# An encoder layer's MLP up stage: products issued as two row tiles of 64 contraction rows

## The chip, the core and the metric

The kernel runs on one core of a Trainium2 chip. The metric is the device time of one execution in microseconds; the profile is one further execution, recorded by the hardware profiler. TensorE (PE in the profile, its weight loads PEld) multiplies into PSUM, a memory of eight banks of 512 fp32 columns on 128 partitions. ScalarE (ACT) and VectorE (DVE) read those banks; GpSimd (POOL) works between buffers of the on-chip memory; SyncE (SP) issues most transfers. Each engine takes its instructions in order.

## What is computed

A layer with two attention branches, followed by a squared-ReLU MLP, for 256 prompt rows and 1024 sample rows of width 1024:

```python
def _layer(x, rel_bias, g_mix, w_in, b_gate, w_branch_a, w_branch_b, w_out, sink, g_mlp, w_up, w_down):
    ...
    x = x + merged @ w_out
    h = _rmsnorm(x, g_mlp)
    return x + jnp.square(jax.nn.relu(h @ w_up)) @ w_down
```

The change is in `h @ w_up`: 1280 rows, 1024 deep, 4096 columns wide.

## The kernel before

Every product is made from operands that are split in a high and a low part of the type fp32r: `hi` is a copy rounded to fp32r (ACT), `lo` is the rest (DVE), and three products, hi by lo, lo by hi and hi by hi, are added up in one PSUM bank. `split_steps` makes such a pair, `six` issues the three products of each piece of 128 contraction rows. Each product loads 128 x 128 weights and passes 512 columns, or 256 for the prompt.

The sample rows go through seven block products in place of eight, each of half depth and half width (the names A11, A12, S1 to S4 and A22 are its combined operands); the prompt's 256 rows are multiplied in the plain way.

The up stage is 16 calls of `up`, called units 0 to 15 here, each for 256 columns of `w_up`. A unit holds seven **runs** of twelve products of 512 columns, made by `seven`, and two prompt sums of 24 products of 256 columns, made by `prompt`. In an ordinary unit PE's order is: A11 into bank x; A12 into y; the prompt's first sum; S2 into x, on top of what is there; S3 into z; S1 into x; A22 into z; S4 into x; the prompt's second sum. Between two runs into the same bank, the sum so far is read out:

- c1: after A11, ACT copies x; `relu2_sum` adds c1 to y on DVE and squares its positive part: the quarter u11.
- c2: after S2, ACT copies x. c7: after S3, ACT copies z.
- u22 is x after S1 plus c7; u21 is z after A22 plus c2 (both on DVE); u12 is x after S4 alone (`relu2`, two ACT instructions).
- the prompt's sums go through `relu2` in halves of 128 columns.

POOL then forms four sums of the quarters, S1 to S4 (L1986 to L1989), and SP stores seven buffers u, which are there once each: the next unit's u11 waits until POOL's third sum has read the old one. Meanwhile the weights of the next unit are prepared by `right_pair`: POOL subtracts to ta and tb (DVE does it for unit 1), ACT makes whi and DVE wlo of four weight tiles per unit, of 128 x 1024 elements. These steps stand between the runs, where `steps_of` takes them from a generator; within one engine the order is that of the program. Unit 0 does more: its hooks (`entering`) split the combined activations (chi on ACT, clo on DVE) and turn the last prompt tile, and it issues the first two runs of unit 1 ahead of its own S4. The last unit's hooks split the first operands of the down stage (dhi and dlo).

PSUM is one pool of eight banks under four tags: three mm, two sc, two pt, one pv. The sum x takes one of mm, y of pt, z of sc, the prompt pv and sc. The down stage, `down.go()`, sums into dn in all eight.

Of the kernel before, what the change touches and what calls it, by code (L numbers as in the profile page):

```python
# [10 lines left out]
F32 = mybir.dt.float32  # L11
F32R = mybir.dt.float32r
AF = mybir.ActivationFunctionType
ALU = mybir.AluOpType
# [83 lines left out]
def encoder_kernel(  # L98
# [25 lines left out]
    psum = ctx.enter_context(tc.tile_pool(name="psum", bufs=1, space=PSUM))  # L124
    narrow, narrows = ExitStack(), []

    def slot(name, shape=(P, D), dt=F32):
# [201 lines left out]
    def turned(t, tags=("pt", "pt")):  # L329

        banks = []
        for h in range(2):
            ps = bank(tags[h], "tr")
            for i in range(4):
                k = 4 * h + i
                nc.tensor.transpose(ps[:, P * i : P * (i + 1)], xn[t][:, P * k : P * (k + 1)], ident)  # L336
            banks.append(ps.rearrange("p (i q) -> p i q", i=4))
        del xn[t]
        return banks

    def six(ps, lefts, rights, first, last, mid=None):

        seq = [x for (lh, ll), (rh, rl) in zip(lefts, rights) for x in ((rl, lh), (rh, ll), (rh, lh))]
        for i, (a, b) in enumerate(seq):
            nc.tensor.matmul(ps, a, b, start=first and i == 0, stop=last and i == len(seq) - 1,  # L345
                             skip_group_check=True)
# [586 lines left out]
    if True:  # L933
# [16 lines left out]
        class Rows:  # L950
# [5 lines left out]
            def begin(self):  # L956
                self.z = stage("long", (P, T), n=4)
# [938 lines left out]
    with ExitStack() as pre:  # L1896
        late = pre.enter_context(tc.tile_pool(name="stage", bufs=1))

        def stage(name, n, bufs=1):
            return late.tile([P, n], F32, name=name, tag=name, bufs=bufs)  # L1900

        def relu2(out, ps):
            nc.scalar.activation(out, ps, AF.Relu)
            nc.scalar.activation(out, out, AF.Square)  # L1904

        def relu2_sum(out, ps, other):
            nc.vector.tensor_tensor(out, ps, other, op=ALU.add)
            nc.vector.scalar_tensor_tensor(out, out, 0.0, out, op0=ALU.max, op1=ALU.mult)

        def begin(parts):  # L1910

            x, y = bank("mm", "x"), bank("pt", "y")
            seven(x, A11, parts[0], 0, last=False)
            c1 = stage("c1", 512)
            nc.scalar.activation(c1, x, AF.Copy)
            yield
            seven(y, A12, parts[0], 1)
            yield x, y, c1

        begun = {}  # L1920
        stores_u = []

        def store_u():
            while stores_u:
                nc.sync.dma_start(*stores_u.pop(0))

        def up(j, b, parts, hooks):

            def prompt_out(ps, dst):
                for i, d in enumerate(dst):
                    relu2(d[:, 512:], ps[:, P * i : P * i + P])

            start = begin(parts)
            if j not in begun:
                next(start)
            z = bank("sc", "z")
            nb = np_ = None
            steps_of(b, 2)  # L1940
            next(hooks, None)
            store_u()
            u = [stage(f"u{i}", TH) for i in range(7)]
            u11, u12, u22, u21 = u[A11], u[A12], u[A22], u[S3]
            x, y, c1 = begun[j] if j in begun else next(start)
            relu2_sum(u11[:, :512], y, c1)
            steps_of(b, 2)
            if j:
                pa = prompt(parts[0])
# [7 lines left out]
            nc.scalar.activation(c2, x, AF.Copy)  # L1957
# [6 lines left out]
            nc.scalar.activation(c7, z, AF.Copy)  # L1964
            if not j:
                steps_of(nb, 2)
            next(hooks, None)
            seven(x, S1, parts[2], 0, False, False)
# [4 lines left out]
            seven(z, A22, parts[2], 1, False)  # L1973
            relu2_sum(u21[:, :512], z, c2)
            next(hooks, None)
            if not j:
                *_, begun[1] = begin(np_)
            seven(x, S4, parts[3], 1, False)
            relu2(u12[:, :512], x)
            next(hooks, None)  # L1980
            if not j:
                steps_of(nb, 4)
                prompt_out(prompt(parts[0]), (u11, u21))
                steps_of(nb, 2)
            prompt_out(prompt(parts[3], "sc"), (u12, u22))
            nc.gpsimd.tensor_tensor(u[S1], u21, u22, op=ALU.add)  # L1986
            nc.gpsimd.tensor_tensor(u[S2], u[S1], u11, op=ALU.subtract)
            nc.gpsimd.tensor_tensor(u[S3], u11, u21, op=ALU.subtract)
            nc.gpsimd.tensor_tensor(u[S4], u12, u[S2], op=ALU.subtract)  # L1989
            stores_u.extend((scr_u[j // 4][:, i, j % 4, :], u[i]) for i in (A11, S1, A22, S2, S3, A12, S4))  # L1990
            next(hooks, None)
            return nb, np_

        def entering():

            run(halves(S3, combined[S3]))
            yield
            run(turn_prompt(9, ("pt", "sc")))
# [8 lines left out]
            yield  # L2007

        b = b0, p0
# [6 lines left out]
        store_u()  # L2016

    down.go()


# [22 lines left out]
```

## Time and profile before

| | |
|---|---|
| median of 3 runs | 1674.7 us (1674.65 to 1675.09) |
| span of the profiled execution, first to last instruction | 1672.7 us |
| granted TensorE clock | 1.000 |
| products (PE), of them in the up stage | 9256, 2112 (84 + 48 in each of 16 units) |
| HBM read, written | 175.13 MB, 90.92 MB |
| waits of PE in the up stage longer than 0.1 us | one, 0.2 us, at its start |

The profile puts a product's record from its start to its modelled end, and products are pipelined: a record of 0.39 us stands every 0.23 us. So the pace is read from the starts. A row of the timeline is: start, length, engine, line, operation, output and inputs, shapes, number of merged instructions, and in brackets how long the engine stood idle before and on what it waited. ACT, DVE and POOL records are lengths that can be added up.

### The profile page before, as it was taken

How to read it: one execution, taken by the hardware profiler on the slowest of the kernel's cores; microseconds unless marked ns; L12 is line 12 of the kernel's file. 1: busy time of each engine (PE TensorE's matmuls, PEld its weight loads, DVE VectorE, ACT ScalarE, POOL GpSimd, SP SyncE). 2: the span in 40 equal slices, each digit the busy share in tenths (PEclk: the TensorE clock that was granted, in tenths of full speed). 3: DMA queues.
4: the chain of work that ended last, by engine and by line, in shares of the span. 5: the costliest groups of instructions: out<-in, count | busy, mean ns of one | idle time of the engine just before them, and what ended most of it. 6: DMA issues, size and time to landing. Idle time of an engine off the chain costs nothing.

```text
span 1672.7 us, 24767 instructions
## 1 busy us (share of the span) xinstructions
PE 1661.8 (99%) x9256; PEld 1413.9 (85%) x9256; DVE 951.1 (57%) x1534; ACT 714.3 (43%) x1473; POOL 494.3 (30%) x372
## 2 busy tenths in 40 slices
PE   9999999999999999999999999999999999999998
PEld 7898888888888888888888888888888888888886
DVE  6732233455654565667278545445456775867665
ACT  6232323345654655654176333333334333333435
POOL 1212222111112352100100656455554250514240
PEclk9999999999999999999999999999999999999999
DMA  7416552666667794845121443343356934733333
GB/s 256 150 54 126 134 132 75 165 196 189 198 184 228 192 236 134 284 135 193 38 89 59 161 160 120 121 161 125 116 191 230 362 113 137 253 104 107 120 120 126
DMA packets 224176, 262.45 MB, mean 157 GB/s; under 512 B 29486, under 2 KB 153694, under 8 KB 224056
## 3 DMA queue, kind: packets, MB, share of 16 engines
q1 hardware_dynamic: 217000, 242.69, 45.4%
q0 software_dynamic: 6720, 17.65, 5.1%
q8 instruction: 73, 1.20, 0.3%
q10 hardware_dynamic: 336, 0.53, 0.1%
q14 instruction: 47, 0.39, 0.1%
HBM read 175.13 MB, written 90.92 MB: 159 GB/s over the span
## 4 chain that ended last, share of the span: by engine, by line
PE 96%; ACT 2%; DVE 1%; DMA 1%; issue 0%; SPq 0%; DVEq 0%; ACTq 0%
PE dn L345 22%; PE x L345 19%; PE mm L192 14%; PE z L345 10%; PE v L819 6%; PE y L345 5%; PE mm L345 5%; PE pv L345 3%; PE sc L345 3%; PE pt L1193 2%; PE pv L1209 2%; PE sc L553 1%; PE pv L600 1%; PE pt L586 1%; PE tr L336 1%; PE sc L1167 1%
## 5 line engine op out<-in xcount | busy, mean ns | idle before, releaser
L345 PE MATMUL dn<-dhi,ulo 128*128 128x512 f32 x448 | 174.3, 389 | 0.0
L345 PE MATMUL dn<-dlo,uhi 128*128 128x512 f32 x448 | 174.3, 389 | 0.0
L345 PE MATMUL dn<-dhi,uhi 128*128 128x512 f32 x448 | 174.3, 389 | 0.0
L345 PE MATMUL x<-chi,wlo 128*128 128x512 f32 x424 | 166.5, 393 | 0.0
L345 PE MATMUL x<-clo,whi 128*128 128x512 f32 x424 | 165.6, 390 | 0.0
L345 PE MATMUL x<-chi,whi 128*128 128x512 f32 x424 | 165.0, 389 | 0.0
L312 DVE TENSOR_TENSOR wlo<-ta,whi 128x1024 fp32r<-128x1024 f32 x30 | 56.3, 1876 | 174.0 <-ACT whi L310 174.0
L312 DVE TENSOR_TENSOR wlo<-raw,whi 128x1024 fp32r<-128x1024 f32 x60 | 89.6, 1494 | 103.1 <-ACT whi L310 98.2
L391 POOL TENSOR_TENSOR tb<-raw 128x512 f32<-128x512 f32 x25 | 32.3, 1290 | 363.7 <-DMA raw<-in_w_in_dram 111.8
L345 PEld LDWEIGHTS dn<-dhi,ulo 128*128 128x128 f32 x448 | 84.1, 188 | 17.6
L345 PEld LDWEIGHTS dn<-dhi,uhi 128*128 128x128 f32 x448 | 84.1, 188 | 17.4
L345 PEld LDWEIGHTS dn<-dlo,uhi 128*128 128x128 f32 x448 | 84.1, 188 | 17.4
L345 PEld LDWEIGHTS x<-chi,whi 128*128 128x128 f32 x424 | 79.6, 188 | 17.1
L345 PEld LDWEIGHTS x<-chi,wlo 128*128 128x128 f32 x424 | 79.8, 188 | 15.1
L345 PEld LDWEIGHTS x<-clo,whi 128*128 128x128 f32 x424 | 79.8, 188 | 14.6
L1735 POOL TENSOR_TENSOR t<-raw,t 128x1024 f32<-128x1024 f32 x16 | 46.4, 2924 | 149.2 <-DMA raw<-in_w_down_dram 149.2
L186 DVE TENSOR_TENSOR ulo<-uraw,uhi 128x1024 fp32r<-128x1024 f32 x56 | 86.1, 1558 | 4.4 <-ACT uhi L185 4.4
L1886 DVE TENSOR_TENSOR v<-v,dn 128x512 f32<-128x512 f32 x90 | 59.7, 683 | 42.3 <-PE dn L345 42.3
L186 DVE TENSOR_TENSOR dlo<-raw,dhi 128x1024 fp32r<-128x1024 f32 x32 | 50.1, 1590 | 46.3 <-ACT dhi L185 45.3
L1986 POOL TENSOR_TENSOR u<-u,u 128x640 f32<-128x640 f32 x16 | 25.1, 1569 | 173.3 <-ACT u L1904 173.3
L345 PE MATMUL dn<-dhi,up 128*128 128x512 f32 x224 | 73.5, 389 | 0.0
L345 PE MATMUL z<-chi,wlo 128*128 128x512 f32 x184 | 71.6, 389 | 0.0
(319 smaller groups left out, 4619.2 us busy)
## 6 DMA issues: line engine op xcount, KB each, us to landing
scr_u<-u SPq DMA_DIRECT2D x112, 320.0 KB, 2.6
uraw<-scr_u SPq DMA_DIRECT2D x56, 512.0 KB, 3.9
raw<-in_w_down_dram SPq DMA_DIRECT2D x36, 512.0 KB, 6.7
raw<-in_w_up_dram SPq DMA_DIRECT2D x32, 512.0 KB, 5.2
raw<-in_w_in_dram SPq DMA_DIRECT2D x25, 512.0 KB, 5.2
sg<-scr_g SPq DMA_DIRECT2D x32, 256.0 KB, 6.2
uraw<-scr_u SPq DMA_DIRECT2D x28, 256.0 KB, 4.5
qk<-scr_kb SPq DMA_DIRECT2D x48, 128.0 KB, 2.6
```

The costliest lines, as they stand in the source:

```text
L186: nc.vector.tensor_tensor(lo, src, hi.bitcast(F32), op=ALU.subtract)
L192: nc.tensor.matmul(ps, a, b, start=i == 0, stop=i == len(seq) - 1)
L312: nc.vector.tensor_tensor(lo, src, hi.bitcast(F32), op=ALU.subtract)
L336: nc.tensor.transpose(ps[:, P * i : P * (i + 1)], xn[t][:, P * k : P * (k + 1)], ident)
L345: nc.tensor.matmul(ps, a, b, start=first and i == 0, stop=last and i == len(seq) - 1, skip_group_check=True)
L391: (nc.vector if vector else nc.gpsimd).tensor_tensor(o, x, y, op=ALU.subtract)
L819: nc.tensor.matmul(ps[:, :n], a, b, start=k == 0 and j == 0, stop=k == KC - 1 and j == 2)
L1193: nc.tensor.transpose(ps[:, P * k : P * k + P], s[:, h, P * b : P * b + P], ident)
L1209: nc.tensor.matmul(pv[HALVES[h], P * i : P * i + P], src, pt[:, at + 2 * b + h, :], start=b == 0, stop=b == W // P - 1, skip_group_check=True)
L1735: nc.gpsimd.tensor_tensor(o, a, b, op=ALU.subtract)
L1886: nc.vector.tensor_tensor(v, v, ps, op=ALU.add)
L1986: nc.gpsimd.tensor_tensor(u[S1], u21, u22, op=ALU.add)
```

## The change

Three things change. A product of 128 contraction rows becomes two products of 64 rows, one on the upper half of the array's rows and one on the lower, issued one after the other, each into a bank of its own (`tiled`). A sum therefore lies in two banks, and is joined where it is read: `closed` copies the first bank on ACT and adds the second on DVE; `relu2_sum` has a second add. And PSUM is held in three pools, one after the other: the old one up to the up stage, one of four double banks a to d in it, and the old layout again for the down stage; a table, HOMES, gives each sum its double bank by unit.

```diff
+    def both_banks(tag, name):
+        return psum.tile([P, 2, 512], F32, name=name, tag=tag, bufs=1)
...
+    def tiled(ps, lefts, rights, n, first, last):
+
+        seq = [x for (lh, ll), (rh, rl) in zip(lefts, rights) for x in ((rl, lh), (rh, ll), (rh, lh))]
+        for i, (a, b) in enumerate(seq):
+            for h, rows in enumerate(HALVES):
+                nc.tensor.matmul(ps[:, h, :n], a[rows, :], b[rows, :], start=first and i == 0,
+                                 stop=last and i == len(seq) - 1, skip_group_check=True)
...
+        def closed(out, ps, n=512):
+
+            nc.scalar.activation(out, ps[:, 0, :n], AF.Copy)
+            nc.vector.tensor_tensor(out, out, ps[:, 1, :n], op=ALU.add)
...
         def relu2_sum(out, ps, other):
-            nc.vector.tensor_tensor(out, ps, other, op=ALU.add)
+            nc.vector.tensor_tensor(out, ps[:, 0, :], other, op=ALU.add)
+            nc.vector.tensor_tensor(out, out, ps[:, 1, :], op=ALU.add)
             nc.vector.scalar_tensor_tensor(out, out, 0.0, out, op0=ALU.max, op1=ALU.mult)
...
+        HOMES = ({"x": "a", "y": "c", "z": "d", "p": "d", "q": "a"}, {"x": "b", "y": "c", "p": "d", "z": "a", "q": "c"},
+                 {"x": "d", "y": "a", "p": "b", "z": "c", "q": "a"})
...
             def prompt_out(ps, dst):
+                c = stage("cp", NP)
+                closed(c, ps, NP)
                 for i, d in enumerate(dst):
-                    relu2(d[:, 512:], ps[:, P * i : P * i + P])
+                    relu2(d[:, 512:], c[:, P * i : P * i + P])
...
-            seven(x, S2, parts[1], 0, False, False)
+            seven_tiled(x, S2, parts[1], 0, False, False)
             c2 = stage("c2", 512)
-            nc.scalar.activation(c2, x, AF.Copy)
+            closed(c2, x)
...
-            seven(z, S3, parts[1], 1, last=False)
+            z = home_of(j, "z")
+            seven_tiled(z, S3, parts[1], 1, last=False)
             c7 = stage("c7", 512)
-            nc.scalar.activation(c7, z, AF.Copy)
+            closed(c7, z)
...
-            seven(x, S4, parts[3], 1, False)
-            relu2(u12[:, :512], x)
+            seven_tiled(x, S4, parts[3], 1, False)
+            closed(u12[:, :512], x)
+            relu2(u12[:, :512], u12[:, :512])
```

How the instructions move is shown at three places. A name in brackets is what the row waits for.

PE, the beginning of z's second run (A22) in the last unit, with the end of x's run S1 ahead of it; x and z are the PSUM sums, chi and clo the split activations, whi and wlo the split weights. Before:

```order
L345 MATMUL x<-clo,whi 128x512
L345 MATMUL x<-chi,whi 128x512
L345 MATMUL z<-chi,wlo 128x512 [waits Activation_49]
L345 MATMUL z<-clo,whi 128x512
L345 MATMUL z<-chi,whi 128x512
```

With the change:

```order
L366 MATMUL x<-clo,whi 128x512 x2
L366 MATMUL x<-chi,whi 128x512 x2
L366 MATMUL z<-chi,wlo 128x512 [waits DVE_49]
L366 MATMUL z<-chi,wlo 128x512
L366 MATMUL z<-clo,whi 128x512 x2
L366 MATMUL z<-chi,whi 128x512 x2
```

Each product stands there twice, once per tile, and the run's first product, which writes z again, waits for DVE where it waited for ACT.

DVE, the middle of an ordinary unit, from u11 to the low parts of the next weights. Before:

```order
L1907 TENSOR_TENSOR u_10420<-y,c_10406 128x512 [waits DMAHW2_49,PE_49,Pool_49]
L1908 SCALAR_TENSOR_TENSOR u_10420<-u_10420 128x512 [waits DVE_49]
L312 TENSOR_TENSOR wlo<-tb,whi 128x1024 [waits Activation_49]
L312 TENSOR_TENSOR wlo<-raw,whi 128x1024 [waits DMAHW1_49,PE_49,Activation_49]
L1907 TENSOR_TENSOR u_10425<-x,c_10508 128x512 [waits DMAHW4_49,PE_49,Activation_49]
L1908 SCALAR_TENSOR_TENSOR u_10425<-u_10425 128x512 [waits DVE_49]
```

With the change:

```order
L1931 TENSOR_TENSOR u_12009<-y,c_11995 128x512 [waits DVE_49,DMAHW4_49,PE_49,Pool_49]
L1932 TENSOR_TENSOR u_12009<-u_12009,y 128x512 [waits DVE_49]
L1933 SCALAR_TENSOR_TENSOR u_12009<-u_12009 128x512 [waits DVE_49]
L322 TENSOR_TENSOR wlo<-tb,whi 128x1024 [waits Activation_49]
L1924 TENSOR_TENSOR c_12124<-c_12124,x 128x512 [waits Activation_49]
L1924 TENSOR_TENSOR cp<-cp,p 128x256 [waits Activation_49]
L322 TENSOR_TENSOR wlo<-raw,whi 128x1024 [waits DMAHW3_49,Activation_49]
L1924 TENSOR_TENSOR c_12163<-c_12163,z 128x512 [waits Activation_49]
L1931 TENSOR_TENSOR u_12014<-x,c_12163 128x512 [waits DMAHW6_49,DVE_49,PE_49]
```

Three closings are new there: c2 (from x), the prompt's (cp, from p) ahead of the low part of raw, and c7 (from z) behind it.

DVE, the beginning of unit 1, from the low part of ta to the low part of raw. Before:

```order
L312 TENSOR_TENSOR wlo<-ta,whi 128x1024 [waits DVE_49,Activation_49]
L312 TENSOR_TENSOR wlo<-tb,whi 128x1024 [waits PE_49,Activation_49]
L1907 TENSOR_TENSOR u_9421<-y,c_9309 128x512 [waits DMAHW5_49,Pool_49]
L1908 SCALAR_TENSOR_TENSOR u_9421<-u_9421 128x512 [waits DVE_49]
L312 TENSOR_TENSOR wlo<-raw,whi 128x1024 [waits Activation_49]
```

With the change:

```order
L1924 TENSOR_TENSOR cp<-cp,p 128x256 [waits Activation_49]
L322 TENSOR_TENSOR wlo<-ta,whi 128x1024 [waits Activation_49]
L1924 TENSOR_TENSOR cp<-cp,q 128x256 [waits DVE_49,Activation_49]
L322 TENSOR_TENSOR wlo<-tb,whi 128x1024 [waits DVE_49,Activation_49]
L1931 TENSOR_TENSOR u_9594<-y,c_9402 128x512 [waits DMAHW5_49,Pool_49]
L1932 TENSOR_TENSOR u_9594<-u_9594,y 128x512 [waits DVE_49]
L1933 SCALAR_TENSOR_TENSOR u_9594<-u_9594 128x512 [waits DVE_49]
L322 TENSOR_TENSOR wlo<-raw,whi 128x1024 [waits Activation_49]
L1924 TENSOR_TENSOR c_9685<-c_9685,x 128x512 [waits Activation_49]
```

Unit 0's two prompt closings (cp from p and from q) now stand around the low part of ta, and unit 1's closing of x (c from x) stands behind u11's three operations, the first of which waits for POOL.

More of the change, by code (lines that the diff above doesn't have):

```diff
@@ L123, in encoder_kernel, with open_banks @@
     slots = ctx.enter_context(tc.tile_pool(name="slots", bufs=N_M))
-    psum = ctx.enter_context(tc.tile_pool(name="psum", bufs=1, space=PSUM))
+    psums = [ctx.enter_context(ExitStack()) for _ in range(3)]
+    def open_banks(i):
+        if i:
+            psums[i - 1].close()
+        return psums[i].enter_context(tc.tile_pool(name=f"psum{i}", bufs=1, space=PSUM))
+    psum = open_banks(0)
     narrow, narrows = ExitStack(), []
@@ L331, in turned @@
         banks = []
+        both = both_banks(tags, "tr") if isinstance(tags, str) else None
         for h in range(2):
-            ps = bank(tags[h], "tr")
+            ps = bank(tags[h], "tr") if both is None else both[:, h, :]
             for i in range(4):
@@ L1931, in prompt_out @@
             def prompt_out(ps, dst):
+                c = stage("cp", NP)
+                closed(c, ps, NP)
                 for i, d in enumerate(dst):
-                    relu2(d[:, 512:], ps[:, P * i : P * i + P])
-            start = begin(parts)
+                    relu2(d[:, 512:], c[:, P * i : P * i + P])
+            start = begin(j, parts)
             if j not in begun:
                 next(start)
-            z = bank("sc", "z")
             nb = np_ = None
@@ L1948, in up @@
             if j:
-                pa = prompt(parts[0])
+                pa = prompt_tiled(parts[0], j, "p")
             if j + 1 < FF // P // 2:
```

37 lines of the change are left out of this document (24 added, 13 removed).

## The prediction

> **What bounds the kernel now.** I read the page's busy times and its chain of waits first, then the busy time by stretch for the up stage, then the chain in order of time and single instructions of one unit.
>
> ```profile
> span 1672.7 us, 24767 instructions
> PE 1661.8 (99%) x9256; PEld 1413.9 (85%) x9256; DVE 951.1 (57%) x1534; ACT 714.3 (43%) x1473; POOL 494.3 (30%) x372
> PE 96%; ACT 2%; DVE 1%; DMA 1%; issue 0%; SPq 0%; DVEq 0%; ACTq 0%
> ```
>
> TensorE is the bound from end to end: 99% busy, and 96% of the chain that ended last. Any wait that PE gets is added to the time whole, and any nanosecond taken from a product comes off whole.
>
> ```profile
> 889.00:912.00 23.00, 22.89 (x105) 19.01 (x106) 22.74 (x24) 16.11 (x21) 0.00 (x0) 1.00 0.20 52
> 1086.00:1111.00 25.00, 25.00 (x136) 21.68 (x135) 12.58 (x10) 8.84 (x17) 13.59 (x8) 1.00 0.41 135
> 889.00:1285.00 396.00, 395.89 (x2109) 343.21 (x2110) 214.60 (x182) 153.92 (x285) 198.18 (x116) 1.00 0.44 146
> ```
>
> The columns after the length are PE, PEld, DVE, ACT and POOL. The up stage, 889 to 1285, is 396 us without a gap on PE, at full clock. An ordinary unit leaves DVE half idle (12.58 of 25 us). Unit 0 does not: DVE works 22.74 of 23 us there.
>
> ```profile
> 1166.26 2.87 PE pv L345 x24
> 1284.99 369.96 PE dn L345 x1632
> ...
> 1097.20 0.39 PE L345 MATMUL z<-chi,wlo 128*128 128x512 f32 x1
> 1097.20 0.19 PEld L345 LDWEIGHTS z<-clo,whi 128*128 128x128 f32 x1
> 1099.92 0.39 PE L345 MATMUL x<-chi,wlo 128*128 128x512 f32 x1
> ```
>
> From the first z product at 1097.20 to the next run at 1099.92 twelve products pass: 226.7 ns each (the down stage: 369.96/1632 = 226.7). A prompt product of 256 columns takes 2.87/24 = 119.6 ns. The difference, 107.1 ns for 256 columns, leaves 12.5 ns per product that do not grow with its width. The weights of the next product load while this one runs: both rows begin at 1097.20.
>
> **Part 1, the pairs.** 2112 products (1344 of 512 columns, 768 of 256) become 2112 pairs of half depth. The multiplications are the same; whether a pair takes as long as the product it replaces decides most. The kernel already has such pairs, in attention, in plain fp32:
>
> ```profile
> 22.53 1.03 PE L336 MATMUL tr<-ident,xn 128*128 128x128 f32 x8
> ...
> 355.86 0.39 PE L345 MATMUL z<-chi,whi 128*128 128x512 f32 x1
> 356.18 1.16 PE L553 MATMUL sc<-qk 64*128 64x128 f32 x16
> ```
>
> The last record of either group lasts 0.27 us, so the eight full products start (1.03 - 0.27)/7 = 108 ns apart. Sixteen tile products one after another would need 15 x 0.108 + 0.27 = 1.89 us; two at a time, with 0.1 us for the first weights, 7 x 0.108 + 0.27 + 0.1 = 1.13. Measured is 1.16. So tiles do run two at a time, loads too, and a pair costs at most 4 ns more than a product. No fp32r tile product stands in this trace. Bounds for its pair: the 12.5 ns vanish altogether (2112 x 12.5 = 26.4 us won), or each tile pays them in turn (26.4 us lost), or tiles don't overlap (2112 products twice: +397 us). I take 1.5 ns more per pair, from the fp32 row: **+3.2 us**. Each tile has the same 512 columns to take through its own rows, and its own change of weights between two products, so I see nothing that a second tile could fill. Four changes between tiled and whole products (two at unit 0's transposes, entry, exit): 355.86 + 0.23 to 356.18 is a gap of 0.09 us; **+0.4**.
>
> The Trainium skill's page "TensorE: Matmul & The Clock Gate", section "Part 3: Packing small matmuls — row/col tiling", says that a weight load overlaps a running product only when its row group differs. By that rule the tiles would hide loads that are now exposed, and the first rival below would hold. This trace disagrees for the bulk of a load: in the same rows a load of 0.19 us and a product of 0.39 us are passed every 0.227 us. At most the 12.5 ns could be of that kind.
>
> **Part 2, the evacuations.** A sum that was one ACT copy or one DVE add is now that and one DVE add more, of the second bank. PE, which writes the same banks again, waits for DVE where it waited for ACT. Work: per unit four closings of 512 columns, three second adds, two closings of 256: 7 x 0.69 + 2 x 0.42 = 5.7 us of DVE. In an ordinary unit DVE has the room. What counts is the order of its queue. One ordinary unit, where the third run (x) ends at E = 1097.20:
>
> ```profile
> 887.43 0.42 DVE L1589 TENSOR_TENSOR s<-s,hraw 128x256 f32<-128x256 f32 x1
> ...
> 1097.40 0.60 ACT L1957 ACTIVATE c<-x 128x512 f32<-128x512 f32 x1 [5.85 <-PE x L345]
> 1097.89 0.27 ACT L1903 ACTIVATE u<-pv 128x128 f32<-128x128 f32 x1
> 1098.92 1.04 ACT L310 ACTIVATE whi<-raw 128x1024 fp32r<-128x1024 f32 x1
> 1099.99 1.22 DVE L312 TENSOR_TENSOR wlo<-raw,whi 128x1024 fp32r<-128x1024 f32 x1 [3.53 <-ACT whi L310]
> 1100.12 0.60 ACT L1964 ACTIVATE c<-z 128x512 f32<-128x512 f32 x1 [0.15 <-PE z L345]
> 1101.57 1.29 POOL L391 TENSOR_TENSOR tb<-raw 128x512 f32<-128x512 f32 x1 [6.78 <-DMA raw<-in_w_up_dram]
> 1102.89 0.69 DVE L1907 TENSOR_TENSOR u<-x,c 128x512 f32<-128x512 f32 x1 [1.68 <-PE x L345]
> 1104.58 2.31 DVE L312 TENSOR_TENSOR wlo<-raw,whi 128x1024 fp32r<-128x1024 f32 x1
> ```
>
> Now the queue is: ACT copies x (E + 0.2 to 0.8) and the prompt's bank (to 1.1); DVE adds x's second bank (0.85 to 1.55) and the prompt's (to 1.95); only then may ACT's four relu instructions go (1.03 us, 1097.89 to 1098.92), then whi (3.0 to 4.05); DVE's wlo stands ahead of z's closing and takes 4.1 to 5.3; z's add ends at 5.9, and PE may write z again at E + 6.0. It would come there after the z and x runs, 24 x 0.2267 = E + 5.45. **Wait: 0.55 us per unit.** The other closings have room: x's own second writing needs E + 1.65 and comes at E + 2.7; the last prompt sum now reaches POOL 2.6 us after its run instead of 1.4, and DVE's chain behind it is done 0.6 us before x's next closing is due. Bounds: 0.2 if each handover is 0.05 faster, 1.4 if POOL's subtractions (1101.57, E + 4.4) come over wlo, as the 2.31 of the next wlo shows; they should move to E + 5.6, since their load is issued behind POOL's later sums. Units 2 to 14: 13 x 0.55 = **+7.2**.
>
> In the last unit two splits of the down stage stand between:
>
> ```profile
> 1273.75 1.99 ACT L185 ACTIVATE dhi<-raw 128x1024 fp32r<-128x1024 f32 x2
> 1275.02 2.36 DVE L186 TENSOR_TENSOR dlo<-raw,dhi 128x1024 fp32r<-128x1024 f32 x2
> ```
>
> z's add then ends 2.3 later, E + 8.2: a wait of 2.8 there: **+2.8**.
>
> **Part 3, units 0 and 1,** where DVE has no room:
>
> ```profile
> 890.68 2.36 DVE L312 TENSOR_TENSOR clo<-s,chi 128x1024 fp32r<-128x1024 f32 x2
> 896.55 2.35 DVE L312 TENSOR_TENSOR clo<-s,chi 128x1024 fp32r<-128x1024 f32 x2
> 898.82 2.36 DVE L312 TENSOR_TENSOR clo<-hraw,chi 128x1024 fp32r<-128x1024 f32 x2
> 913.96 0.69 DVE L391 TENSOR_TENSOR tb<-raw,ta 128x512 f32<-128x512 f32 x1
> 924.75 0.69 DVE L1907 TENSOR_TENSOR u<-y,c 128x512 f32<-128x512 f32 x1 [2.98 <-POOL u L1988]
> 925.47 1.32 DVE L1908 SCALAR_TENSOR_TENSOR u<-u 128x512 f32<-128x512 f32 x1
> 926.71 1.21 DVE L312 TENSOR_TENSOR wlo<-raw,whi 128x1024 fp32r<-128x1024 f32 x1
> ...
> 892.80 0.48 PE L345 MATMUL x<-chi,wlo 128*128 128x512 f32 x1
> 898.34 0.39 PE L345 MATMUL x<-chi,wlo 128*128 128x512 f32 x1
> 926.04 0.39 PE L345 MATMUL x<-chi,wlo 128*128 128x512 f32 x1
> ...
> 916.04 1.04 ACT L310 ACTIVATE whi<-ta 128x1024 fp32r<-128x1024 f32 x1
> ...
> 919.10 1.59 POOL L1986 TENSOR_TENSOR u<-u,u 128x640 f32<-128x640 f32 x1 [106.85 <-ACT u L1904]
> ```
>
> x's first closing stands behind the clo pair that ends at 893.04: done 893.7, where PE started at 892.80: +0.9. x's second closing stands behind the pair that ended at 898.90 and behind 1.4 us of new adds: done 901.0; PE, at 898.34 + 0.9, waits +1.8. z's closing, behind the pair that ended at 901.18: +0.1. PE's next four runs find their sums closed. By tb's last subtraction (end 914.65) DVE carries eight new adds, 5.5 us, so the prompt's closing ends at 920.5. ACT's relu waits for it, and ACT's whi<-ta stands behind: 921.7 instead of 916.04; its wlo ends at 924.0 where unit 1's third run could start at 923.5: +0.6. Behind wlo comes the second prompt's closing (924.4), then its relu, so POOL starts at 925.6 instead of 919.10. u11's add of unit 1 waits for POOL's third sum, 5.65 later as before: 931.2. It holds DVE's queue: three operations (2.7), wlo (1.2), and x's closing ends at 935.8. PE, due at 926.04 + 3.4 = 929.4, waits: +6.4. In the kernel before, that closing was a copy on ACT, and DVE's wait of 2.98 us cost nothing. Together **+9.8**, 3 either way.
>
> **Sum:** 3.2 + 0.4 + 7.2 + 2.8 + 9.8 = 23.4 us on the profiled span of 1672.7, which is 2.0 under the median 1674.7: 1672.7 + 23.4 + 2.0 = **1698 us**, 1.4% slower. Its own range, from pairs at 0 to 4 ns, unit waits of 0.2 to 1.4 and 3 us on units 0 and 1, is 1688 to 1717.
>
> **Rivals.** *The fixed part is hidden (faster).* If the 12.5 ns are a change of weights that the other tile covers, a pair costs 12.5 less and 2 more: 2112 x 10.5 = 22.2 us won, 1.39 per unit. But the walk of the queues doesn't shorten: a unit's two runs take 0.25 less, its wait becomes 0.8, so units 2 to 14 win 7.7, the last loses 1.7, units 0 and 1, paced by DVE, lose 9.1: +3.5 with the changes of tiling, 1678. It is faster than before only if my waits are smaller: with none, 1653. It turns at 22 us of waits. For it: nobody has named what the 12.5 ns are. Against it: the fp32 pairs gain nothing.
> *Each tile pays the fixed part.* +26.4; the runs give z's closing 0.3 more, so 0.25 per unit, 2.5 and 9.8 remain: 26.4 + 3.3 + 2.5 + 9.8 + 0.4 = 42.4, 1717. For it: tiles might change weights one after the other. Against it: 1.16 us above.
> *fp32r tiles don't overlap, so the change does not do what it says.* 1344 x 0.2267 + 768 x 0.1196 = 397, with the waits covered: 2071. Only that no fp32r tile stands in the trace speaks for it.
>
> **How the numbers follow.** Forecast 69%, hidden part 16%, paid twice 11%, no overlap 4%. The time is the forecast's, 1698. The range 1677 to 1719 leaves out the lower ten points of the hidden part, the 4, three of the 11 and three of the forecast's tails. A measurement of this kernel tells about 0.2%, 3.3 us. Faster by more: 9 of the 16 and two of the forecast's lower tail, 11%; within: 5 and 2, 7%; slower: 82%.
>
> **What would show it.** A product pair of 512 columns should pass every 227 to 231 ns in the changed kernel's trace, one of 256 every 120 to 124. In an ordinary unit PE should be idle about 0.5 us ahead of z's second run, with DVE's add of c<-c,z as the releaser, and some 6 us in unit 1 ahead of x's run, behind u11's wait for POOL. A pair at 216 ns, or no such waits, would prove the forecast wrong; so would pairs at 240, or at twice the time.

## The result and the profile after

The changed kernel takes **1705.3 us** (median of 4 runs, 1702.75 to 1705.96) against 1674.9 (1674.65 to 1675.69) for the kernel before in the same session: ratio 1.0179, 95% interval 1.0164 to 1.0193. It is slower by 30 us. The profiled execution took 1702.75 us, its span is 1701.0 against 1672.7. From the page of the changed kernel, busy times:

```profile
span 1701.0 us, 29153 instructions
PE 1670.0 (98%) x11368; PEld 1416.2 (83%) x11368; DVE 1023.7 (60%) x1678; ACT 736.7 (43%) x1521; POOL 495.3 (29%) x372
```

PE's busy time rose by 8 us, the span by 28: most of the loss is idle time of PE. DVE has 144 instructions and 73 us more. The busy time by stretch, from the first product of the up stage to the first of the down stage, shows where all of it lies; first the kernel before, then the changed one. Behind the length and the busy times of PE, PEld, DVE, ACT and POOL stand the granted clock, the DMA's share and GB/s:

```profile
885.98:1284.83 398.85, 398.70 (x2123) 345.20 (x2122) 217.52 (x189) 155.79 (x288) 198.18 (x116) 1.00 0.44 146
```

```profile
889.02:1312.98 423.96, 406.83 (x4233) 347.99 (x4233) 284.68 (x326) 175.18 (x332) 197.19 (x116) 0.99 0.42 137
```

The stage begins 3.0 us later and is 25.1 us longer: 28.15 of the 28.3. The waits of PE there, the one at its entry included, by what ended them (total, times, longest):

```profile
PE z L366 <- DVE c L1924: 10.5, 14, 3.3
PE x L366 <- DVE c L1924: 5.4, 1, 5.4
PE x L366 <- ACT praw L1579: 3.4, 1, 3.4
PE dn L356 <- DVE cp L1924: 1.2, 1, 1.2
```

Where there was one wait of 0.2 us there are now seventeen with 20.5 us, all at handovers of PSUM banks. I take them in turn.

**An ordinary unit**, in the timeline of the changed kernel; here E, the end of the third run, is 1062.94. Rows in between are left out, here and below:

```profile
1062.94 0.39 PE L366 MATMUL z<-chi,wlo 64*128 64x512 f32 x2
1063.80 0.68 DVE L1924 TENSOR_TENSOR c<-c,x 128x512 f32<-128x512 f32 x1
1064.39 0.41 DVE L1924 TENSOR_TENSOR cp<-cp,p 128x256 f32<-128x256 f32 x1
1065.66 0.39 PE L366 MATMUL x<-chi,wlo 64*128 64x512 f32 x2
1065.78 0.31 ACT L1928 ACTIVATE u<-u 128x128 f32<-128x128 f32 x1
1065.99 1.05 ACT L320 ACTIVATE whi<-raw 128x1024 fp32r<-128x1024 f32 x1
1067.07 1.23 DVE L322 TENSOR_TENSOR wlo<-raw,whi 128x1024 fp32r<-128x1024 f32 x1 [2.26 <-ACT whi L320]
1068.16 0.39 PE L366 MATMUL x<-chi,whi 64*128 64x512 f32 x2
1068.21 0.68 DVE L1924 TENSOR_TENSOR c<-c,z 128x512 f32<-128x512 f32 x1
1068.95 0.50 PE L366 MATMUL z<-chi,wlo 64*128 64x512 f32 x2 [0.40 <-DVE c L1924]
1069.28 0.40 PE L366 MATMUL z<-clo,whi 64*128 64x512 f32 x2
```

Two things are to be seen. Twelve pairs pass from 1062.94 to 1065.66: 226.7 ns each, what a whole product took. And the forecast's chain stands there link by link: the prompt's add, ACT's relus, whi, wlo, z's add, and z's run at E + 6.01. Its last predecessor began at 1068.16, so without a wait it would have begun at 1068.39: it lost 0.56 us. The idle time in brackets says 0.40, since it counts from the modelled end of the last product; the starts count. Then the second pair follows after 0.33 in place of 0.227, and the whole run takes 2.85 in place of 2.72: a run that starts after a wait loses another 0.13.

Eight of the thirteen units 2 to 14 wait like this one; five wait longer. In the longest of them E is 1267.83:

```profile
1266.34 0.69 DVE L1931 TENSOR_TENSOR u<-y,c 128x512 f32<-128x512 f32 x1 [2.98 <-POOL u L2031]
1268.40 1.22 DVE L322 TENSOR_TENSOR wlo<-tb,whi 128x1024 fp32r<-128x1024 f32 x1
1269.53 0.68 DVE L1924 TENSOR_TENSOR c<-c,x 128x512 f32<-128x512 f32 x1
```

x's closing begins at E + 1.70 there, not at E + 0.86: it stands behind the low part of tb, that one behind u11, and u11 waits for POOL's third sum. The rest of the chain moves with it.

**Unit 1:**

```profile
932.37 0.69 DVE L1931 TENSOR_TENSOR u<-y,c 128x512 f32<-128x512 f32 x1 [2.95 <-POOL u L2031]
934.43 1.22 DVE L322 TENSOR_TENSOR wlo<-raw,whi 128x1024 fp32r<-128x1024 f32 x1
935.56 0.68 DVE L1924 TENSOR_TENSOR c<-c,x 128x512 f32<-128x512 f32 x1
936.30 0.80 PE L366 MATMUL x<-chi,wlo 64*128 64x512 f32 x2 [5.38 <-DVE c L1924]
936.89 0.63 PE L366 MATMUL x<-clo,whi 64*128 64x512 f32 x2
937.31 0.63 PE L366 MATMUL x<-chi,whi 64*128 64x512 f32 x2
939.83 0.40 PE L366 MATMUL x<-chi,whi 64*128 64x512 f32 x2
```

x's closing stands behind u11, which waits for POOL, as forecast. After 5.4 idle microseconds the pairs come every 0.43 us instead of 0.227, for some 3.5 us: the granted clock has fallen to a half.

**The entry**, which the prediction had not seen:

```profile
887.91 1.06 ACT L1579 ACTIVATE praw<-tr 128x512 f32<-128x512 f32 x2
889.02 0.79 PE L366 MATMUL x<-chi,wlo 64*128 64x512 f32 x2 [3.39 <-ACT praw L1579]
889.62 0.63 PE L366 MATMUL x<-clo,whi 64*128 64x512 f32 x2
```

praw are ACT's copies of a prompt tile's transposes. In the kernel before, x took a bank of another tag (mm) than the transposes (pt) and did not wait for them. Now its banks belong to a new pool, and its first product waits for these copies, the last readers of the old pool. Which banks of PSUM x got, the trace doesn't tell. This wait too is followed by products at half the clock.

### The profile page after: what moved, and what is told of

It is laid out like the page before. It is cut to its first block, busy times and chain, and to the rows that moved or that the text cites. A ratio compares the mean times of both kernels' runs of the same rounds, so it can differ in the third digit from the quotient of the medians.

```text
span 1701.0 us, 29153 instructions
## 1 busy us (share of the span) xinstructions
PE 1670.0 (98%) x11368; PEld 1416.2 (83%) x11368; DVE 1023.7 (60%) x1678; ACT 736.7 (43%) x1521; POOL 495.3 (29%) x372
## 5 line engine op out<-in xcount | busy, mean ns | idle before, releaser
L410 POOL TENSOR_TENSOR tb<-raw 128x512 f32<-128x512 f32 x25 | 32.3, 1294 | 367.8 <-DMA raw<-in_w_in_dram 131.8
L366 PE MATMUL x<-chi,wlo 64*128 64x512 f32 x512 | 102.4, 395 | 8.8 <-DVE c L1924 5.4
L366 PE MATMUL x<-clo,whi 64*128 64x512 f32 x512 | 101.6, 392 | 0.0
L366 PE MATMUL x<-chi,whi 64*128 64x512 f32 x512 | 101.1, 390 | 0.0
L322 DVE TENSOR_TENSOR wlo<-ta,whi 128x1024 fp32r<-128x1024 f32 x30 | 43.5, 1450 | 82.0 <-ACT whi L320 82.0
L195 ACT ACTIVATE dhi<-raw 128x1024 fp32r<-128x1024 f32 x32 | 33.5, 1058 | 88.5 <-PE dn L356 88.1
L640 POOL DMA_DIRECT2D scr_b<-o x44 | 23.9, 546 | 152.9 <-DVE o L282 88.7
L320 ACT ACTIVATE whi<-raw 128x1024 fp32r<-128x1024 f32 x60 | 63.0, 1051 | 11.1 <-DVE wlo L322 10.6
L356 PE MATMUL x<-chi,wlo 128*128 128x512 f32 x168 | 66.4, 395 | 0.0
```

The costliest lines, as they stand in the source:

```text
L195: nc.scalar.activation(hi, src, AF.Copy)
L320: nc.scalar.activation(hi, src, AF.Copy)
L322: nc.vector.tensor_tensor(lo, src, hi.bitcast(F32), op=ALU.subtract)
L366: nc.tensor.matmul(ps[:, h, :n], a[rows, :], b[rows, :], start=first and i == 0, stop=last and i == len(seq) - 1, skip_group_check=True)
L410: (nc.vector if vector else nc.gpsimd).tensor_tensor(o, x, y, op=ALU.subtract)
L640: nc.gpsimd.dma_start(scr_b[g][i][:, qa : qa + nq], o[:, c : c + nq])
```

## The experiments

All times are medians beside the kernel before, which took 1674.0 to 1675.0 us in these sessions. The table reads the stages from the starts of PE's rows: from x's first product to the first of unit 2, from there to the first of the last unit, and from there to the first dn product.

| run | units 0, 1 | units 2 to 14 | last unit | sum | time (ratio, 95%) |
|---|---|---|---|---|---|
| before | 51.1 | 322.9 | 24.8 | 398.9 | |
| after | 60.0 | 334.1 | 29.8 | 424.0 | 1705.3 (1.0164 to 1.0193) |
| e1, whole products | 60.7 | 332.3 | 30.9 | 423.9 | 1704.0 (1.0147 to 1.0190) |
| e2, no second adds | 51.0 | 322.9 | 25.9 | 399.8 | 1682.1 (1.0029 to 1.0054) |
| e3, split behind c7 | 60.9 | 327.4 | 30.6 | 418.9 | 1703.4 (1.0137 to 1.0185) |
| e4, prompt behind c7 | 60.4 | 324.7 | 28.9 | 413.9 | 1692.8 (1.0082 to 1.0119) |
| e5, u11 behind c2 | 58.1 | 333.1 | 32.3 | 423.4 | 1702.9 (1.0156 to 1.0195) |
| e6, praw first | 60.5 | 332.9 | 31.0 | 424.4 | 1702.6 (1.0159 to 1.0190) |
| e8, all moved | 55.0 | 324.7 | 29.1 | 408.8 | 1688.5 (1.0068 to 1.0094) |
| e9, e8 mended | 54.2 | 325.0 | 30.5 | 409.7 | 1686.4 (1.0058 to 1.0085) |

### Pairs or waits: whole products in two banks

My theory: a pair costs what a product cost, and all the time is in the handovers. The rivals: the pairs themselves cost or win something.

```diff
-            for h, rows in enumerate(HALVES):
-                nc.tensor.matmul(ps[:, h, :n], a[rows, :], b[rows, :], start=first and i == 0, ...)
+            nc.tensor.matmul(ps[:, i % 2, :n], a, b, start=first and i < 2, ...)
```

> The changed kernel with whole products of 128 rows again, piece after piece in turn into the two banks; pools, banks, closings and their order stay. Theory A (a pair costs what a product costs, and the time is lost in waits for the second bank's add): whole products every 226.7 ns as the pairs, the same wait of about 0.56 us ahead of z's second run, 3.5 us in the last unit, 5.5 us in unit 1, and 1705 us within 2. Rival B (the pairs themselves cost something, the 1.5 ns of the forecast or more): the waits stay, and the time falls by 3 us or more, to 1702 or below. Rival C (pairs gain something that the waits hide): whole products are slower than the pairs were, and the time rises above 1708. At the slow clock of the entry a whole product should also take 0.427 us, the time of 512 columns, if the 12.5 ns are hidden there.

1704.0 us, and 423.9 us for the stage, 0.05 us from the changed kernel's. The waits of PE:

```profile
PE z L365 <- DVE c L1923: 8.5, 14, 3.1
PE x L365 <- DVE c L1923: 5.3, 1, 5.3
```

Not one tile is left in the up stage, and the loss stands. The tiles are therefore not its cause; what stayed is, the two banks per sum with their closings and the new pools. The totals agree better than their parts, by luck: in units 2 to 14 only one wait is longer than 0.56 us here, which saves 1.8 us, and in the last unit the clock fell once more. At the entry a whole product took 0.427 us at the half clock, the same as a pair.

### The pairs alone: only the first bank is read

```diff
             nc.scalar.activation(out, ps[:, 0, :n], AF.Copy)
-            nc.vector.tensor_tensor(out, out, ps[:, 1, :n], op=ALU.add)
```

So in the three other readers of a sum as well.

> The tiles stay, but only the first bank of each sum is read: every add of a second bank is left out, so half of every sum of the up stage is left out of the result. Theory A: without those adds no wait is left but that at the entry (3.0 us of waiting and 1.1 us at a slow clock), so the pairs alone show their price: 1679 to 1680 us if they cost nothing, 227 ns per pair. Rival B (pairs cost 1.5 ns more): 1682 to 1683. Rival C (the fixed 12.5 ns are hidden in the pairs where no wait holds them): 1653 to 1660, pairs every 214 to 216 ns.

The chain in order of time, in one unit:

```profile
1072.71 2.75 PE x L366 x24
1075.46 2.72 PE z L366 x24
1078.18 2.72 PE x L366 x24
1080.90 2.72 PE z L366 x24
1083.62 2.72 PE x L366 x24
1086.34 2.87 PE q L366 x48
```

The same 2.72 and 2.87 as whole products had, and units 2 to 14 take 322.92 us, as in the kernel before, to the hundredth. The pace decides for theory A. The time alone would not: the profiled execution took 1678.5, a little under theory A's 1679 to 1680, but the median of ten, 1682.1, lies in rival B's range. The ten lie between 1678.5 and 1687.2, those above 1683 with a mean granted clock of 0.995 to 0.997 where the shortest had 0.999. The entry's wait is 3.4 us in this kernel too, and whether the clock falls after it changes from execution to execution (here, in the profiled one, it didn't: x's first run took 2.86 us, not 4.22). One more wait is left, which theory A had not named: 0.9 us ahead of the down stage, where the third pool begins.

### The chain of an ordinary unit, link by link

First the split (wlo, and the last unit's dlo) behind z's closing, then, in another kernel, the prompt's closing and relus behind it:

```diff
             if j:
                 prompt_out(pa, (u11, u21))
-            steps_of(b, 2)
-            next(hooks, None)
+            else:
+                steps_of(b, 2)
+                next(hooks, None)
             z = home_of(j, "z")
             ...
             closed(c7, z)
+            if j:
+                steps_of(b, 2)
+                next(hooks, None)
```

> In units 1 to 15 the last split of the next weights (whi and wlo from raw), and in the last unit the two splits of the down stage, are issued behind z's closing instead of ahead of it. Theory A (the wait ahead of z's second run is the chain prompt's add, relus, whi, wlo, z's add): no wait there in units 2 to 15: 11 us of units 2 to 14 and 3.6 of the last come back, 1690 to 1692 us. Rival B (the wait is set by the handover of z's own copy and add, not by what stands ahead): the 0.56 us stay, 1705. Rival C (the split now comes too late for x's fourth run, S4): a new wait of up to 1 us ahead of S4 in each unit takes the place of the old, 1700 or above.

```diff
-            if j:
-                prompt_out(pa, (u11, u21))
             steps_of(b, 2)
             ...
             closed(c7, z)
+            if j:
+                prompt_out(pa, (u11, u21))
```

> The other link of the same chain: the split stays where it is, but the closing of the prompt's first sum and its four relu instructions are issued behind z's closing. Theory A (the chain needs both links: ACT's relus wait for DVE's add of the prompt's second bank, and hold up whi): without them whi goes 1.4 us earlier, the 0.56 us wait of units 2 to 14 is gone, and the last unit's wait falls from 3.5 to about 2.1 us: 1692 to 1694 us. Rival B (the split alone is the cause): the wait stays in units 2 to 14, about 1703.

The waits in the second of them, from unit 2 on:

```profile
PE dn L356 <- DVE cp L1924: 1.7, 1, 1.7
PE z L366 <- DVE c L1924: 1.6, 1, 1.6
```

Ahead of z's second run the split's move leaves no wait, the prompt's move one, in the last unit (1.6 us); units 2 to 14 win back 6.7 us by the first and 9.4 by the second, of 11.2. So the chain needs both links, as theory A said, and neither is enough alone. The expected sizes hold for the prompt's move (1692.8, of 1692 to 1694). For the split's move they don't: 1703.4 instead of 1690 to 1692. Its median lies 4.6 us above its profiled execution (1698.8), the four runs spread over 6.7 us, and even the profile has only 5.0 us back. There the runs S1, A22 and S4 of most units take 0.04 to 0.18 us longer than 2.72; what holds them I have not shown. And in the last unit x's fourth run waits 2.1 us for u22's add, which now stands behind dlo: the wait moved one run on, rival C at one place.

### Unit 1: u11 behind x's closing

```diff
-            relu2_sum(u11[:, :512], y, c1)
+            if j != 1:
+                relu2_sum(u11[:, :512], y, c1)
...
             closed(c2, x)
+            if j == 1:
+                relu2_sum(u11[:, :512], y, c1)
```

> In unit 1 alone, u11's three operations on DVE, the first of which waits for POOL's third sum, are issued behind x's closing c2 instead of ahead of it. Theory A (x's run waits 5.5 us because the closing stands behind an add that waits for POOL, and the wait lets the clock fall, which costs another 1.7 us): the wait ahead of x's run is gone and its run is back to about 2.75 us at full clock; but u11 now stands ahead of z's closing, which it releases at about the same moment as it released x's, 936.7, where z's second run is due at 933.5: a wait of about 3.2 us there. Units 0 and 1 fall from 60.0 us to about 56, the time to about 1701. Rival B (x's run waits for its own handover or for POOL itself): the 5.5 us stay where they are, 1705.

x's wait falls from 5.4 to 1.7 us and its run is back at full clock; z's second run waits 2.8 instead (3.2 expected). The 1.7 that stay I had missed: the split of raw also stands ahead of x's closing on DVE. Units 0 and 1 win 2.0 us, half of what was expected. The time doesn't show it: in this execution the clock fell in the last unit, after its wait of 3.3 us, and z's run there took 5.3 us instead of 2.86.

### The entry: the copies of praw first

```diff
-                next(turning, None)
+                steps_of(turning, 2 if t == 9 else 1)
                 nc.vector.tensor_tensor(x2[t][:, sl], x2[t][:, sl], ps, op=ALU.add)
```

> Ahead of the up stage, ACT's copies of the eighth prompt tile's transposes (praw) are issued ahead of the square of the last row tile, which waits for DVE. Theory A (the new pool makes x's first product wait for the last reader of the old pool, these copies; the wait of 3.4 us lets the clock fall in some executions): x's first run starts 1.1 to 1.2 us behind the transposes' end, about 1.9 us earlier than in the changed kernel, and takes 2.9 us instead of 4.2, so that y's run begins about 3 us earlier; unit 0's closings, behind DVE's queue, then hold PE for some of the 0.9 and 1.8 us of the forecast, so that units 0 and 1 together win less than 3 us: 1702 to 1704 us. Rival B (the pool makes it wait for something else, or the start is bound by the first split): x's start stays at about 889, 1705.

x's first run starts 2.04 us behind the transposes' start instead of 4.41 (0.79 in the kernel before), and takes 2.81 us instead of 4.22. So these readers of the old pool do hold it. What remains is the next such reader, DVE's add of the residual rows, also called x, from the old pool's bank mm:

```profile
PE x L366 <- DVE x L1681: 1.0, 1, 1.0
```

Whether the pool as a whole is the barrier, or only banks that x now shares with both tags, these runs don't separate. And now, in unit 0, the run of x behind S3 starts 1.4 us late: the wait that the prediction had put at 1.8 there, and which the longer wait at the entry had hidden. From the transposes to unit 2 1.9 us are won; the median is 2.7 us lower, which the intervals can't tell from nothing.

### All of it at once

The prompt's closing of e4, u11 of unit 1 behind z's closing, the copies of e6, and the last unit's splits behind u22; then the same with two places mended:

```diff
-            next(hooks, None)
+            steps_of(hooks, 1 if j < last else 3)
             seven_tiled(x, S2, parts[1], 0, False, False)
             ...
             closed(c2, x)
-            steps_of(b, 2)
+            steps_of(b, 4 if j == 1 else 2)
```

> Tiles stay; all that the runs so far point to is moved at once: the prompt's first closing behind z's closing in units 1 to 15, unit 1's u11 behind z's closing, the last unit's splits for the down stage behind u22, and the copies of praw ahead of the square. Theory A (the change costs nothing but its waits, which lie at four places): units 2 to 14 take 323 to 325 us as in the kernel before, the last 26 to 27, units 0 and 1 52 to 55, and the whole 1677 to 1683 us: not faster than before, since the pairs win nothing. Rival B (the pairs have a gain of their own that the waits hid): below 1671. Rival C (the waits only move on to the next closing): 1688 or above.

> As the run with all waits moved, with its two mishaps mended: in unit 1 the split of raw is issued behind x's closing too, and in the last unit the splits dhi and dlo are issued ahead of x's closing c2, while DVE has room, so that the prompt's last closing isn't late for the down stage. Theory A (the change costs nothing but waits): the wait of 1.8 us in unit 1 is gone, the one ahead of the down stage is 1.2 to 1.4 us instead of 4.2, the stretch from x's first run to the first dn product falls from 408.8 to 403.5 to 404.5 us (398.9 in the kernel before), and the time to 1681 to 1684. Rival B (the moves only push a wait on): no less than 407, 1686 or above.

1688.5 and 1686.4 us: 17 and 19 of the 30 us are back, less than expected both times. In the first, 1.4 us stay in unit 0, 1.8 in unit 1, and the down stage waits 4.2 us, since DVE's queue ended in dlo, ulo (the low part of a stored buffer u) and only then the prompt's last closing; behind that wait the clock falls, and the down stage is 1.6 us longer, which the table doesn't hold. In the second the 1.8 us of unit 1 are gone, but x's fourth run waits 1.05 us there for u22's add. In its last unit the dlo that was to be early comes behind u11, and so behind POOL:

```profile
1276.03 0.69 DVE L1931 TENSOR_TENSOR u<-y,c 128x512 f32<-128x512 f32 x1 [3.00 <-POOL u L2036]
1279.22 2.35 DVE L196 TENSOR_TENSOR dlo<-raw,dhi 128x1024 fp32r<-128x1024 f32 x2
1281.49 0.68 DVE L1924 TENSOR_TENSOR c<-c,x 128x512 f32<-128x512 f32 x1
1282.22 0.50 PE L366 MATMUL x<-chi,wlo 64*128 64x512 f32 x2 [2.09 <-DVE c L1924]
1283.43 0.63 PE L366 MATMUL x<-clo,whi 64*128 64x512 f32 x2
```

PE waits 2.1 us for x, and even after that the clock falls for a run. Rival B, that waits move on, holds in the units where DVE is full; theory A holds in units 2 to 14, where 1.8 to 2.1 us are left. No version beats the kernel before, and none could by moving waits: without any in units 2 to 14 the pairs only reach its time (e2).

### What makes two tiles run at once

```diff
         for i, (a, b) in enumerate(seq):
-            for h, rows in enumerate(HALVES):
-                nc.tensor.matmul(...)
+            pass
+        for h, rows in enumerate(HALVES):
+            for i, (a, b) in enumerate(seq):
+                nc.tensor.matmul(...)
```

> All twelve (or 24) products of the upper 64 rows of a sum are issued first, into the first bank, and then those of the lower rows, into the second. Theory A (two products run at once only because neighbours in the queue lie on different halves of the array's rows, and each pays the whole time of its columns and the 12.5 ns): 226.7 and 119.6 ns per product of half depth as for whole ones, twice the time of a pair: an ordinary unit takes 2 x 24.8 us, the waits of units 2 to 15 are covered by the longer runs, and the whole time is 2070 to 2085 us. Rival B (half-depth products lack the 12.5 ns when nothing runs beside them): 214 and 107 ns, about 2030 us. Rival C (the hardware finds the pairs in its queue by itself): no slower than 1705.

2375.2 us: no theory had that. The timeline at the end of one run's lower half (x) and the beginning of the next run's upper half (z), and a window of the stage, with the granted clock third from its end:

```profile
1005.63 0.62 PE L368 MATMUL x<-chi,whi 64*128 64x512 f32 x1
1005.64 0.79 PE L368 MATMUL z<-chi,wlo 64*128 64x512 f32 x1
1006.06 0.62 PE L368 MATMUL x<-chi,wlo 64*128 64x512 f32 x1
1006.24 0.62 PE L368 MATMUL z<-clo,whi 64*128 64x512 f32 x1
```

```profile
1000.00:1500.00 500.00, 500.00 (x1938) 436.51 (x1936) 107.70 (x142) 75.38 (x145) 78.08 (x56) 0.50 0.14 47
```

The granted clock is 0.50 through the stage, and products of one half come every 0.427 us. But at each change of halves the next half starts early: z's first product begins together with the fourth-last of x, and three of x begin behind it. Two kernels separate these things. Groups of four products per half in turn:

> The changed kernel with the tiles issued in groups: four products of the upper 64 rows, then the four of the lower rows, then the next four of the upper. Not alternated at all, the up stage took about 7.2 us per run at half the granted clock, in which 24 products took the time of 16.8, as if 3.6 products were passed at once at each change of halves. Theory A (TensorE starts a product on the free half when it is up to some four places behind the one that runs): groups of four overlap almost whole, at full clock, 2.7 to 3.2 us per run, 1705 to 1760 us. Rival B (only direct neighbours overlap, one product at each change of halves): 8 products in the time of 7, a run takes 4.8 us or more at full clock, 9 at the half, and the time is above 1950.

1707.3 us (ratio 1.0176 to 1.0214), full clock: as good as pairs. And the upper half alone, with e2's closings:

> Only the tiles of the upper 64 rows are issued, into the first bank, which alone is read; the lower half of every contraction in the up stage is left out, so there are 2112 products of half depth and no second adds. It asks why the run whose tiles were not alternated had half the granted clock through the whole up stage. Theory A (the clock stays down while only half of the array's rows are at work, once a wait has let it fall): granted clock 0.5 from the entry to the end of the up stage, 427 and 214 ns per product, the stage takes 1344 x 0.427 + 768 x 0.214 = 738 us instead of 396, the time is about 2015 to 2025 us. If the entry's wait doesn't let the clock fall in this execution, theory A has it fall on its own. Rival B (the low clock came from something else in that run, as the changes between halves): full clock, 226.7 and 119.6 ns if a half-depth product has the whole fixed part, 1679 to 1684 us; 214 and 107 ns if it hasn't, about 1655.

```profile
889.54 0.49 PE L366 MATMUL x<-chi,wlo 64*128 64x512 f32 x1 [3.37 <-ACT praw L1579]
889.88 0.39 PE L366 MATMUL x<-clo,whi 64*128 64x512 f32 x1
890.11 0.45 PE L366 MATMUL x<-chi,whi 64*128 64x512 f32 x1
890.36 0.62 PE L366 MATMUL x<-chi,wlo 64*128 64x512 f32 x1
890.78 0.62 PE L366 MATMUL x<-clo,whi 64*128 64x512 f32 x1
```

```profile
1000.00:1600.00 600.00, 600.00 (x1720) 491.23 (x1719) 121.69 (x130) 114.59 (x221) 144.24 (x104) 0.50 0.24 78
```

2023.1 us, as theory A said. The first products still run at full clock; 0.8 us into the run it falls, as behind other waits (in e9 as late), but here it doesn't come back before the down stage, with PE 600.00 of 600.00 us busy. Both kernels with long stretches on one half have it, and the one with groups of four hasn't. So the low clock goes with an idle half of the array; that the idle half is what keeps it down is my reading, since no run had half the rows at work with no wait ahead.

## Why the forecast came out as it did

The forecast was slower, 1698 us, by pairs at no gain and by waits at four places. Slower it is, for these reasons; the sum was 7 us short. Of these, 4.8 are in the terms below; the other 2.3 are the step from the profiled span to the median, 2.0 us in the forecast and 4.3 here. The three executions that were not profiled had a mean granted clock of 0.994 to 0.995, the profiled one 0.996. (The bounds of the forecast's own range give 1687 at the lower end, not 1688.) The terms, against the profile:

| term | forecast | measured |
|---|---|---|
| Part 1, the pairs | +3.2 | 0.0 (e1, e2) |
| Part 1, changes of tiling | +0.4 | 0.2 at the transposes of unit 0, counted in Part 3; the rest hidden by the entry's wait |
| Part 2, units 2 to 14 | +7.2 | +11.2 |
| Part 2, last unit | +2.8 | +5.0 |
| Part 3, units 0 and 1 | +9.8 | +12.0 (entry 3.0, units 8.9) |
| sum | 23.4 | 28.2 of 28.3 |

**Part 1** held in its mechanism: the tiles overlap, and a pair takes what the whole product took, its 12.5 ns included. Only the 1.5 ns taken over from the fp32 pairs were wrong: an fp32r pair costs nothing. By the rule of the Trainium skill's page "TensorE: Matmul & The Clock Gate", section "Part 3: Packing small matmuls — row/col tiling", a load overlaps only on other rows, so the tiles should have freed something; 226.7 ns before and after disagree with it, as the rows of the prediction did. The same section of the Trainium skill also lets a load into the background weight buffer go ahead. The prediction left that out; it would fit 226.7 ns before and after, and no run here shows that buffer.

**Part 2** had the chain right: z's add was to end at E + 5.9 and PE to start at E + 6.0, and it did at 6.01; the wait was forecast at 0.55 and is 0.56 in eight of thirteen units. Two sizes were missed. A run that starts late loses 0.13 to 0.17 more, 1.9 us over the units. And five units wait longer (0.68 to 1.41 us), for 2.0 more. The walk had DVE add x's second bank at E + 0.85; in these five it begins at E + 0.97 to 1.70, behind the low part of tb and u11's wait for POOL. This is Part 3's mechanism, which the prediction saw in unit 1 alone. In the last unit z waited 3.5 us and lost 0.1 after it, 3.6 where the forecast had 2.8; and the end of the stage had no term at all: the down stage's first bank waits for the prompt's last closing (+1.4). In e2, which has no closings, 1.0 of this stays, so most of it comes with the change of pools.

**Part 3** had its largest step right: u11's wait for POOL holds x's closing, and PE waits 5.5 us (forecast 6.4). Missed was what follows, a clock at half for one run (+1.7). Of the small steps of unit 0 (0.9, 1.8, 0.1, 0.6) only the last showed, as 0.2, since the new pool makes PE wait ahead of all of them and then run at half clock, and in that time DVE catches up; e6 brought one of them out. So the 8.9 us came near the forecast's 9.8 in part by luck: some 3 us of half clock (x's first run took 1.4 us more than in e2, unit 1's run 1.7 more) stand where 3.2 us of small steps fell away. The entry's 3.0 us are by the span; counted from the transposes, which began 0.6 us earlier in this execution, they are 3.6. The part on the change named three pools, and the prediction priced only their tiling; that the first product of a new pool waits for the last reader of the old one is the step that was left out.

The rival with the fixed part hidden falls by e2 (226.7 ns, not 214 to 216), that with the part paid twice by the same row, and that without overlap by both. What e2 adds is that there is no turning point: with no waits at all this change would be worth nothing, so no order of the queues could have made it a gain.

## What to carry to other kernels

Splitting a full-depth product into two row tiles left the time of its columns as it was here (226.7 ns), with nothing to win, and it doubled what must be read out of PSUM. When an evacuation goes from one engine to two, write down the queue of the second engine at each place where the bank is written again: what stands ahead there, and what that waits for, is the new price, and a wait that cost nothing on an idle engine costs everything once a bank hangs on it. A new PSUM pool acted as a barrier as well, at the entry and ahead of the down stage: look for the last reader of the old one.

## What the runs showed of the hardware

- With only 64 of the array's 128 rows at work the granted clock, once at a half, stayed there, though PE was busy without a gap (0.50 over 600 us in e11). The Trainium skill's page "TensorE: Matmul & The Clock Gate", section "What's actually happening", ties the clock to how busy PE has been lately; a stage that the profile calls 100% busy ran at the half here, so by this run more counts than the profile's busy time.
- Waits of 2.1 to 5.4 us were often, not always, followed by a stretch at half the granted clock, of 3.41 us or of twice that (6.83, in unit 1 of the changed kernel and in the last unit of e5). It came behind 2.1 us in e9, and did not behind 2.8 us in unit 1 of e5, 3.3 in the changed kernel's last unit and 3.4 at e2's entry. That is an unsteady price, 1.7 us for unit 1's run, on top of such a wait.
- Products on different halves of the rows overlap when they stand up to four places apart (e7, e10), and one that comes later in the program starts first: z at 1005.64, x's next at 1006.06 (e7). The Trainium skill's page "TensorE: Matmul & The Clock Gate", section "Part 3: Packing small matmuls — row/col tiling", has products start and end in strict order; these rows don't, and the order in which each engine is said above to take its instructions does not hold for the starts of these products.
- The 12.5 ns that an fp32r product has beyond its columns are there for whole products, and for pairs (226.7 ns at 512 columns, 119.6 at 256), and vanish at the half clock: 427 and 213 ns, in proportion to the columns.
